# A one-layer streaming encoder step: when the sample tokens' cross attention, one spreading of a norm and the last norm's scalings are issued

## The chip, the core and the metric

The kernel runs on one core of a Trainium2 chip. The core has a matrix engine (TensorE, PE in the profile, with its weight loads as PEld), a vector engine (DVE), a scalar engine (ACT), a general engine (POOL) and a queue engine that only issues transfers (SP). ACT and POOL can issue transfers too. Each engine works through its own list of instructions in order and waits on semaphores for the others. The metric is the time of one execution on the device, in microseconds (us); lower is better. Three runs of the kernel before have a median of 2162.29 us (2162.05 to 2165.18).

## What is computed

One layer over 1024 prompt tokens and 64 sample tokens (1088 columns in all, D_MODEL 1024): a combined projection, retention and sliding-window attention as two gated branches, a mixing projection, cross attention over 256 memory tokens with 4 heads, a SwiGLU, and a final RMSNorm. What the change touches, cut from the reference:

```python
def rms_norm(x, g=None):
    xf = x.astype(jnp.float32)
    y = xf * lax.rsqrt(jnp.mean(xf * xf, axis=-1, keepdims=True) + EPS)
    if g is not None:
        y = y * g.astype(jnp.float32)
    return y.astype(x.dtype)
...
# x += CrossAttn(RMSNorm(x), memory K/V)   (4 heads, 256 memory tokens)
# x += SwiGLU(RMSNorm(x)), then a final RMSNorm
```

The prompt tokens attend to keys and values projected from the prompt's memory; the sample tokens attend to keys and values from a cache.

## The kernel before, in words

Activations lie with features on the 128 partitions and tokens along the columns. Matrix products are made of fp32r halves: a value is split into a rounded high part (an ACT copy, L124) and the remainder (a DVE subtraction, L125), and each block takes three multiplications (high by high, high by low, low by high: L157 to L159, or L223 to L226 in the large products). A scheduler orders each engine's list; `issue_after` and `in_order` pin an instruction behind the last multiplication, so what is emitted after a product comes after it on TensorE. `self.later` is a list of small steps; `run_later` (L169) empties it after the next product. So whoever appends to `self.later` gets its work placed between two products.

**Cross phase** (`cross_phase`, `attend`). `attend(h)` runs over the heads. It queues the loads of two query weight blocks (`raw`, split to `wq`) and of this head's memory keys and values (`mraw`, split to `mkv`), and then walks `CQ`, the chunks of 256 prompt columns; one chunk has 64 further columns, the sample tokens. A chunk is: two query products (`pd`), the scaled queries (`qf`, split to `cqs`), scores (`css`), softmax (`small_softmax`, L1297 to L1304), four transpositions (`cpt`, copied to `cpT`), the weighted values (`cpo`), and the split of those into `co`. After the last chunk of a head, L1350 to L1369 attend for the sample tokens: the cached keys and values `ck` and `cv` are loaded, scores `csss` (L1355), softmax to `ps`, two transpositions `cpts` (L1360), a DVE copy `cpTs` (L1362), and `cpos` (L1366), whose split goes to `co`. After the last head the output projection reads `co`.

**The norm behind it.** The norm ahead of the SwiGLU needs the factor of every token spread over the partitions. `spread_both` (L364) does this with 12 multiplications by the identity (L369) into a pair of banks, which ACT copies to `rstd_f` (L372, two copies). It is the first of the steps in `self.later` when `gate_up` makes its first large product through `plain` (L246). That product is four quarters of 24 multiplications each; three quarters have their first parts, then their second parts, and the steps run after the third second part (L262). The fourth quarter follows, on the operand `b`.

**Finish** (`finish`, L1702). The last projection's remaining half runs as 16 products of 9 multiplications: column groups c = 0 and c = 1, 272 columns each, with 8 row blocks each. c = 2, the other 544 columns, is done already. After each product `grow` adds it to the residual on DVE (L1721) and squares the result on ACT (L1725); `gather` adds the square of the product before on DVE (L1730). `sums` adds the squares over partitions by multiplications with ones (L1739), `roots` makes the factors in small DVE steps with one ACT square root (L1824 to L1831), `spread` lays them over the partitions (L1757, copied by ACT at L1761 where `copied`). `scale` multiplies a row block by gain and factor in one DVE instruction (L1767) and stores it; `gain` and `aside` do the same in two halves, the gain on ACT (L1772) and the factor on POOL (L1776).

Of the kernel before, what the change touches and what calls it, by code (L numbers as in the profile page):

```python
# [11 lines left out]
F32 = mybir.dt.float32  # L12
# [7 lines left out]
P = 128  # L20
# [89 lines left out]
class Kernel:  # L110
# [132 lines left out]
    def plain(self, w, x, emit, early=None, second=None):  # L243
# [14 lines left out]
        for i, t in emits:  # L258
            out.append(part(i, t, 1))
            if second is not None and len(out) == 1:  # L260
                second(emit(i, t, out[0], None))
# [1022 lines left out]
    def cross_phase(self):  # L1284
        nc, tc, io = self.nc, self.tc, self.io
        mm = nc.tensor.matmul
        with ExitStack() as ctx:
# [17 lines left out]

            def attend(h):
# [10 lines left out]
                for c0, n in CQ:  # L1317
# [32 lines left out]
                ck, cv = t2("ck"), t2("cv")  # L1350
                self.load(ck, io["cmkT"][h])
                self.load(cv, io["cmv"][h])
                pss = pc.tile([P, 2, 256], F32, tag="s", bufs=2, name="csss")
                for dt in range(2):
                    mm(pss[:SMP, 0, :], qsm[:, dt, :], ck[:, dt, :], start=dt == 0, stop=dt == 1)  # L1355
                p = t2("ps")
                small_softmax(pss, SMP, 1, p)
                pt = pc.tile([P, 2, 256], F32, tag="t", bufs=1, name="cpts")
                for kt in range(2):
                    nc.tensor.transpose(pt[:, kt, :SMP], p[:SMP, 0, kt * P:(kt + 1) * P], self.ident[:SMP, :SMP])  # L1360
                pT = cp.tile([P, 2, SMP], F32, tag="pTs", bufs=1, name="cpTs")
                nc.vector.tensor_copy(pT, pt[:, :, :SMP])  # L1362
                po = pc.tile([P, 2, 256], F32, tag="o", bufs=2, name="cpos")
                for dt in range(2):
                    for kt in range(2):
                        mm(po[:, dt, :SMP], cv[:, kt, dt * P:(dt + 1) * P], pT[:, kt, :], start=kt == 0, stop=kt == 1)  # L1366
                for dt in range(2):
                    o = outs[h][dt]
                    self.split(po[:, dt, :SMP], o[:, 0, SEQ:T], o[:, 1, SEQ:T])  # L1369
# [332 lines left out]
    def finish(self, y, rest):  # L1702
# [29 lines left out]
        def sums(c, *more):  # L1732
# [4 lines left out]
            for i, (a, w) in enumerate(spans):  # L1737
                for j, x in enumerate(parts):
                    self.last_mm = nc.tensor.matmul(ps[:, i, :], x[:, a:a + w], self.ones[:, :2], start=j == 0,  # L1739
                                                    stop=j == len(parts) - 1).ins  # L1740
# [28 lines left out]

        def gain(c, k):  # L1770
# [7 lines left out]

        for j in range(2 * KT):
# [23 lines left out]
        spare = [rest[i][0] for i in range(KT - 4, KT - 1)]  # L1803
        scale(0, 0, pb0)
        scale(0, 1, pb0)
# [96 lines left out]
```

## Time and profile before

| | us |
|---|---|
| Median of 3 runs | 2162.29 |
| The profiled execution's own time | 2162.52 |
| Its span | 2160.7 |
| Mean granted TensorE clock in it | 0.997 |
| PE busy | 2134.5 |
| DVE busy | 1552.6 |
| ACT busy | 874.8 |
| POOL busy | 530.4 |

A row of the timeline has the start in us from the span's start, the length in us, the engine, the line, the operation, output and inputs, their shape, and how many instructions were put together (x). Brackets give the idle time of that engine just before and what ended it. Matmuls overlap, so the distance from one start to the next, not the length, is what one costs. The view of waits sums such idle time by what ended it.

The cross phase lies at about 1168 to 1345 us, the spreading at 1449 us, the finish at 2121 us to the end.

### The profile page before, as it was taken

Reading aid. Unit: us, or ns where it says so; the run is one execution under the profiler, and the core shown is the slowest. Engines: PE = TensorE matmul, PEld = TensorE weight load, DVE = VectorE, ACT = ScalarE, POOL = GpSimd, SP = SyncE. Lnnn points to the kernel's source line nnn. Section 1 sums busy time; section 2 is a strip of 40 time slices with the busy share of each in tenths; the row PEclk is TensorE's granted clock in tenths of the full one; section 3 lists DMA queues with packets and bytes.
Section 4 is the critical chain, followed back from the end, with each engine's and each line's share of the span. In section 5 each row is a group of like instructions: output and inputs, shape, how many; then the busy total and the mean of one; then the engine's idle time right before and its main releaser. Section 6 shows DMA issues by size and latency. Waiting matters only on the chain.

```text
span 2160.7 us, 41729 instructions
## 1 busy us (share of the span) xinstructions
PE 2134.5 (99%) x16371; PEld 2082.7 (96%) x16371; DVE 1552.6 (72%) x2912; ACT 874.8 (40%) x1894; POOL 530.4 (25%) x448
## 2 busy tenths in 40 slices
PE   9999999999999999999999999999999999999997
PEld 9999999999999997889999999999999999999997
DVE  8987979776677567656455555677777777777597
ACT  8344434344444356543233333343223222334243
POOL 0000000022343135540000000015565556423531
PEclk9999999999999999999999999999999999999998
DMA  7334444435345485336442122413342332484333
GB/s 262 126 126 123 129 145 134 128 114 160 113 140 190 158 260 184 120 116 207 142 142 78 50 64 68 145 58 105 123 147 91 101 132 82 132 298 158 106 116 113
DMA packets 169893, 290.85 MB, mean 135 GB/s; under 512 B 39266, under 2 KB 96546, under 8 KB 169698
## 3 DMA queue, kind: packets, MB, share of 16 engines
q1 hardware_dynamic: 161666, 269.02, 38.8%
q0 software_dynamic: 3424, 10.82, 1.4%
q10 hardware_dynamic: 4608, 8.36, 1.0%
q8 instruction: 129, 2.11, 0.4%
q14 instruction: 66, 0.54, 0.1%
HBM read 196.97 MB, written 91.16 MB: 133 GB/s over the span
## 4 chain that ended last, share of the span: by engine, by line
PE 85%; DVE 7%; DMA 3%; issue 2%; ACT 2%; POOL 1%; SPq 0%; POOLq 0%; DVEq 0%; ACTq 0%
PE pq L226 17%; PE pq L224 16%; PE pq L223 16%; PE pd L157 8%; PE pd L159 8%; PE pd L158 8%; DVE wq L125 2%; DMA hl<-d_op 1%; PE pss L1005 1%; PE pout L1075 1%; DVE T L125 1%; PE pk L766 1%; PE pp L1051 1%; DVE B L125 1%; PE po L159 1%
## 5 line engine op out<-in xcount | busy, mean ns | idle before, releaser
L124 ACT CAST wq<-raw 128x512 fp32r<-128x512 f32 (+1 forms) x499 | 302.0, 614 | 564.7 <-PE pq L226 220.1
L125 DVE TENSOR_TENSOR wq<-raw,wq 128x512 fp32r<-128x512 f32 (+1 forms) x499 | 426.6, 859 | 137.3 <-ACT wq L124 133.9
L224 PE MATMUL pq<-T,wq 128*128 128x272 f32 x1832 | 492.1, 288 | 0.5 <-DVE T L125 0.5
L223 PE MATMUL pq<-T,wq 128*128 128x272 f32 x1832 | 490.4, 287 | 1.6 <-ACT wq L124 0.6
L224 PE MATMUL pq<-B,wq 128*128 128x272 f32 x1592 | 427.3, 288 | 1.9 <-DVE B L125 1.9
L223 PE MATMUL pq<-B,wq 128*128 128x272 f32 x1592 | 425.6, 287 | 0.2 <-ACT B L124 0.2
L226 PE MATMUL pq<-T,wq 128*128 128x272 f32 x1832 | 382.7, 289 | 1.9 <-DVE wq L125 1.9
L201 POOL TENSOR_TENSOR raw<-raw 128x512 f32<-128x512 f32 (+1 forms) x44 | 62.9, 1429 | 1260.5 <-DVE wq L125 527.6
L223 PEld LDWEIGHTS pq<-T,wq 128*128 128x128 f32 x1832 | 344.3, 188 | 3.2 <-ACT xsq L499 1.2
L224 PEld LDWEIGHTS pq<-T,wq 128*128 128x128 f32 x1832 | 343.9, 188 | 1.5 <-issue 0.7
L226 PE MATMUL pq<-B,wq 128*128 128x272 f32 x1592 | 331.9, 289 | 0.0
L224 PEld LDWEIGHTS pq<-B,wq 128*128 128x128 f32 x1592 | 298.9, 188 | 3.4 <-DVE B L125 3.0
L223 PEld LDWEIGHTS pq<-B,wq 128*128 128x128 f32 x1592 | 298.9, 188 | 0.7 <-ACT B L124 0.4
L226 PEld LDWEIGHTS pq<-T,wq 128*128 128x128 f32 x1832 | 289.6, 189 | 3.6 <-DVE wq L125 2.4
L226 PEld LDWEIGHTS pq<-B,wq 128*128 128x128 f32 x1592 | 251.7, 189 | 0.9 <-issue 0.7
L274 DVE TENSOR_TENSOR u<-pq,u 128x544 f32<-128x544 f32 x177 | 127.1, 718 | 76.0 <-PE pq L226 75.5
L613 DVE TENSOR_TENSOR stage<-pq,u 128x544 f32<-128x544 f32 x112 | 80.1, 717 | 32.5 <-PE pq L226 26.7
L157 PE MATMUL pd<-xc,wq 128*128 128x256 f32 (+1 forms) x256 | 74.5, 291 | 0.0
L159 PE MATMUL pd<-xc,wq 128*128 128x256 f32 (+1 forms) x256 | 74.0, 289 | 0.0
L158 PE MATMUL pd<-xc,wq 128*128 128x256 f32 (+1 forms) x256 | 73.7, 288 | 0.0
L1550 POOL TENSOR_TENSOR stage<-stage,rstd_f 128x544 f32<-128x544 f32 x40 | 63.9, 1608 | 39.1 <-ACT stage L1549 39.1
L204 POOL TENSOR_TENSOR raw<-raw 128x512 f32<-128x512 f32 (+1 forms) x44 | 59.0, 1340 | 53.1 <-DVE wq L125 50.5
(388 smaller groups left out, 4508.9 us busy)
## 6 DMA issues: line engine op xcount, KB each, us to landing
hl<-d_op SPq DMA_DIRECT2D x85, 272.0 KB, 5.3
d_qkv<-stage SPq DMA_DIRECT2D x44, 272.0 KB, 2.3
d_op<-stage SPq DMA_DIRECT2D x44, 272.0 KB, 2.2
d_op<-ht SPq DMA_DIRECT2D x44, 272.0 KB, 3.3
raw<-w_gate SPq DMA_DIRECT2D x22, 512.0 KB, 3.5
raw<-w_up SPq DMA_DIRECT2D x22, 512.0 KB, 5.0
raw<-w_down SPq DMA_DIRECT2D x16, 512.0 KB, 4.8
d_gate<-stage ACTq DMA_DIRECT2D x28, 272.0 KB, 2.8
```

The lines of the kernel that those rows point to most:

```text
L124: self.last_cast = self.nc.scalar.copy(hi, src).ins
L125: return self.nc.vector.tensor_tensor(out=lo, in0=src, in1=hi.bitcast(F32), op=ALU.subtract).ins
L157: mm(ps, wh, xh, start=start, stop=False)
L158: mm(ps, wh, xl, start=False, stop=False)
L159: self.last_mm = mm(ps, wl, xh, start=False, stop=stop).ins
L201: tt(out=a11, in0=a11, in1=a21, op=sub)
L223: mm(ps[:, c, :HC], w[:, 0, ks], x[:, 0, cs], start=start, stop=False)
L224: mm(ps[:, c, :HC], w[:, 0, ks], x[:, 1, cs], start=False, stop=False)
L226: self.last_mm = mm(ps[:, c, :HC], w[:, 1, ks], x[:, 0, c * HC:(c + 1) * HC], start=False, stop=stop).ins
L274: add = lambda out, a, b: nc.vector.tensor_tensor(out=out, in0=a, in1=b, op=ALU.add)
L613: nc.vector.tensor_tensor(out=o, in0=ps, in1=sb, op=ALU.add)
L1550: nc.gpsimd.tensor_tensor(out=g, in0=g, in1=r[t], op=ALU.mult)
```

## The change

Three edits, all of them about when and where work is done.

- **Sample tokens.** `attend` no longer ends with the sample tokens' attention. A new function `sample(h, qsm)` loads `ck` and `cv` and puts three steps into `self.later`, one after the other: scores and softmax, transpositions and copy, weighted values. Each comes after the next query product. `ck`, `cv` and `ps` get a buffer of their own each, where before they took turns in a ring of four. The last head walks its chunks in another order, so that chunks are left behind its sample columns.
- **Spreading.** `plain` runs the steps once more, after the second of the three second parts.
- **Finish.** In `sums` all spans of one operand come before those of the next. From the tenth of the sixteen products on, `gather` of the product before stands ahead of `grow` instead of behind it. Of the eight row blocks of c = 2, DVE scales four within the loop (before: seven) and a fifth after it; three are done by ACT and POOL early in the loop (before: one, at the loop's end). Of c = 0, the last two row blocks go to ACT and POOL, for which ACT also copies the spread factors. Their stores are issued by POOL. The ACT gains of c = 1 come later.

```diff
@@ plain
             out.append(part(i, t, 1))
+            if early is not None and second is None and len(out) == 2:
+                with self.tc.issue_after(self.last_mm):
+                    self.run_later()
...
@@ cross_phase
+            def sample(h, qsm):
+                ck, cv, p = (cp.tile([P, 2, 256], F32, tag=t, bufs=1, name=t) for t in ("ck", "cv", "ps"))
+                self.load(ck, io["cmkT"][h])
+                self.load(cv, io["cmv"][h])
+
+                def scores():
+                    pss = pc.tile([P, 2, 256], F32, tag="s", bufs=2, name="csss")
...
+                    small_softmax(pss, SMP, 1, p)
+                    behind(turn)
+
+                def turn():
...
+                    nc.vector.tensor_copy(pT, pt[:, :, :SMP])
+                    behind(lambda: weigh(pT))
+
+                def weigh(pT):
...
+                behind = lambda f: self.later.append(lambda: self.in_order(f))
+                behind(scores)
...
-                for c0, n in CQ:
+                for c0, n in CQ if h < H - 1 else CQ[3:] + CQ[:3]:
...
+                        sample(h, qsm)
...
-                ck, cv = t2("ck"), t2("cv")
-                self.load(ck, io["cmkT"][h])
...
-                    self.split(po[:, dt, :SMP], o[:, 0, SEQ:T], o[:, 1, SEQ:T])
@@ finish
-            for i, (a, w) in enumerate(spans):
-                for j, x in enumerate(parts):
...
+            steps = [(x, i, a, w) for x in parts for i, (a, w) in enumerate(spans)]
+            for j, (x, i, a, w) in enumerate(steps):
...
+        def turn(j):
+            if (j - 1) % KT and j:
+                gather((j - 1) // KT, rest[(j - 1) % KT][0])
...
+        held = (KT - 2, KT - 1)
         for j in range(2 * KT):
             c, m = divmod(j, KT)
             ps = self.in_order(lambda: product(c, *rest[m]))
+            if j > KT + 1:
+                turn(j)
             grow(c, rest[m][0], ps)
-            if (j - 1) % KT and j:
-                gather((j - 1) // KT, rest[(j - 1) % KT][0])
+            if j <= KT + 1:
+                turn(j)
...
-                pb0 = self.in_order(lambda: spread(0, False))[:, :HC]
-            if c and m < KT - 1:
-                scale(2, m)
-            if c and KT - 5 < m < KT - 1:
-                gain(1, rest[m][0])
-            if j == 2 * KT - 2:
-                gain(2, KT - 1)
-                aside(2, KT - 1)
+                pb0 = self.in_order(lambda: spread(0))[:, :HC]
+                gain(1, spare[0])
+                for k in held:
+                    aside(0, k, nc.gpsimd)
+            if c and m in (0, 1, 2, 4):
+                scale(2, min(m, 3))
+            if c and 0 < m < 4:
+                gain(2, KT - 4 + m)
+                aside(2, KT - 4 + m, nc.gpsimd)
+            if c and 4 <= m < 6:
+                gain(0, held[m - 4])
...
         scale(0, 1, pb0)
+        scale(2, KT - 4)
         self.in_order(lambda: sums(1, squares[1, m]))
         roots(1, lambda: scale(0, 2, pb0))
-        for k in range(3, KT):
+        for k in range(3, held[0]):
             scale(0, k, pb0)
```

What this does to the engines' lists, at three places. The numbers behind names tell tiles of one name apart.

On TensorE, at the end of the first head's last chunk, the instructions before (the next head's first product follows `cpos`):

```order
 L159 MATMUL pd<-xc_13014,wq 128x256
-L1338 MATMUL cpt<-ident,p 128x128
-L1355 MATMUL csss<-ck,qsm 64x256 x2
-L1338 MATMUL cpt<-ident,p 128x128 x3
...
-L1360 MATMUL cpts<-ident,ps 128x64 x2
-L1366 MATMUL cpos<-cpTs,cv 128x64 x4
```

In the changed kernel the two `csss` stand further up, among that chunk's `css`, `cpo` and `pd` rows, `cpts` stands inside the next head's products, and `cpos` some 50 rows behind `cpts`. Between the second `csss` and the first `css` of the next head lie 51 rows. On SP, whose loads start in order, this piece of the difference is the loads between the first and the third head:

```order
 L118 DMA ck<-cmkT 128x512
-L118 DMA cv<-cmv 128x512
 L118 DMA mraw<-d_mk 128x512
 L118 DMA mraw<-d_mv 128x512
+L118 DMA cv<-cmv 128x512
 L118 DMA raw<-w_cq 128x1024
 L118 DMA raw<-w_co 128x1024
```

The load of `ck` in its first row is the second head's now (before: the first head's). With one buffer for `ck` it waits until the first head's `csss` have read theirs, and the next head's `mraw` stands behind it; `cv` waits likewise for `cpos`.

On TensorE in `gate_up`'s first product, around the spreading (L369 before, L372 of the changed kernel). It moves from behind the 24 multiplications of the third second part (operands `B_16831` and `B_16832`) to ahead of them:

```order
 L226 MATMUL pq<-B_16830,wq 128x272 x2
+L372 MATMUL pq<-ident,rs_r 128x128 x6
 L223 MATMUL pq<-B_16831,wq 128x272
...
 L226 MATMUL pq<-B_16832,wq 128x272 x2
-L369 MATMUL pq<-ident,rs_r 128x128 x6
 L223 MATMUL pq<-b_15869,wq 128x272
```

On DVE in the finish, from the last `scale` of c = 2 within the loop to the sum for c = 1, before:

```order
-L1767 SCALAR_TENSOR_TENSOR y_22086<-y_22086,gains,rstd 128x544
-L1721 TENSOR_TENSOR y_22087<-pq,y_22087 128x272
-L1730 TENSOR_TENSOR rstd<-rstd,sq 128x272
-L1767 SCALAR_TENSOR_TENSOR y_22087<-y_22087,gains,rstd 128x544
-L1721 TENSOR_TENSOR y_22088<-pq,y_22088 128x272
-L1730 TENSOR_TENSOR rstd<-rstd,sq 128x272
-L1767 SCALAR_TENSOR_TENSOR rstd_f<-rstd_f,gains,pq 128x272
```

and the same stretch now (L1746 is `gather`, L1737 `grow`, L1783 `scale`):

```order
+L1746 TENSOR_TENSOR rstd<-rstd,sq 128x272
+L1737 TENSOR_TENSOR y_22087<-pq,y_22087 128x272
+L1746 TENSOR_TENSOR rstd<-rstd,sq 128x272
+L1737 TENSOR_TENSOR y_22088<-pq,y_22088 128x272
+L1783 SCALAR_TENSOR_TENSOR rstd_f<-rstd_f,gains,pq 128x272
+L1783 SCALAR_TENSOR_TENSOR y_22084<-y_22084,gains,pq 128x272
+L1783 SCALAR_TENSOR_TENSOR y_22085<-y_22085,gains,rstd 128x544
```

The scalings of 544 columns between the additions are gone, and each `gather` stands ahead of the next `grow`. POOL's list for the finish now reads:

```order
L1796 TENSOR_TENSOR y_22086<-y_22086,rstd 128x544 [waits DVE_49,Activation_49]
L1796 TENSOR_TENSOR y_22087<-y_22087,rstd 128x544
L1796 TENSOR_TENSOR y_22088<-y_22088,rstd 128x544 [waits PE_49]
L1797 DMA o_y<-y_22086 128x544 [waits Pool_49]
L1797 DMA o_y<-y_22087 128x544 [waits DMASW7_49,Pool_49]
L1797 DMA o_y<-y_22088 128x544 [waits Pool_49]
L1796 TENSOR_TENSOR y_22087<-y_22087,rstd 128x272 [waits Activation_49]
L1796 TENSOR_TENSOR y_22088<-y_22088,rstd 128x272
L1797 DMA o_y<-y_22087 128x272 [waits Pool_49]
L1797 DMA o_y<-y_22088 128x272 [waits DMASW2_49,Pool_49]
L1796 TENSOR_TENSOR y_22085<-y_22085,rstd 128x272 [waits Activation_49]
```

Before, it had one multiplication of 544 columns and three of 272 there, and no stores.

More of the change, by code (lines that the diff above doesn't have):

```diff
@@ L1349, in attend @@
                         self.split(po[:, dt, :], o[:, 0, c0:c0 + 256], o[:, 1, c0:c0 + 256])
-                ck, cv = t2("ck"), t2("cv")
-                self.load(ck, io["cmkT"][h])
[L1352 to L1368, printed above, removed]
-                    self.split(po[:, dt, :SMP], o[:, 0, SEQ:T], o[:, 1, SEQ:T])
             for h in range(H):
@@ L1736, in sums @@
             parts = [self.rstd[:, cols[c]], *more]
-            for i, (a, w) in enumerate(spans):
-                for j, x in enumerate(parts):
-                    self.last_mm = nc.tensor.matmul(ps[:, i, :], x[:, a:a + w], self.ones[:, :2], start=j == 0,
-                                                    stop=j == len(parts) - 1).ins
+            steps = [(x, i, a, w) for x in parts for i, (a, w) in enumerate(spans)]
+            for j, (x, i, a, w) in enumerate(steps):
+                self.last_mm = nc.tensor.matmul(ps[:, i, :], x[:, a:a + w], self.ones[:, :2], start=j == 0,
+                                                stop=j == len(steps) - 1).ins
             r = self.np.tile([P, 5], F32, tag="rf", bufs=2, name="rs_f")[:, :len(spans)]
@@ L1777, in aside @@
             queue.dma_start(self.io["o_y"][k, :, cols[c]], o)
+        spare = [rest[i][0] for i in range(KT - 4, KT - 1)]
+        held = (KT - 2, KT - 1)
         for j in range(2 * KT):
```

16 lines of the change are left out of this document (15 added, 1 removed).

## The prediction

> **What bounds the kernel now.** I read the page first, then the view of TensorE's waits from the cross phase on, then the timelines of the three places that the edits touch.
>
> ```profile
> span 2160.7 us, 41729 instructions
> PE 2134.5 (99%) x16371; PEld 2082.7 (96%) x16371; DVE 1552.6 (72%) x2912; ACT 874.8 (40%) x1894; POOL 530.4 (25%) x448
> PE 85%; DVE 7%; DMA 3%; issue 2%; ACT 2%; POOL 1%; SPq 0%; POOLq 0%; DVEq 0%; ACTq 0%
> ```
>
> TensorE sets the time: it is busy for all but 26 us of the span and has 85% of the chain that ended last. The change removes no multiplication, so it can only win where TensorE stands still, and behind its last product. The waits show how much there is to win:
>
> ```profile
> PE pq L1739 <- DVE rstd L1730: 2.4, 1, 2.4
> PE cpos L1366 <- DVE cpTs L1362: 1.7, 4, 0.6
> PE pq L1757 <- DVE rs_f L1831: 1.3, 1, 1.3
> PE pq L223 <- ACT rstd_f L372: 0.9, 1, 0.9
> PE cpo L157 <- ACT cpT L124: 0.7, 1, 0.7
> PE cpo L158 <- DVE cden L1302: 0.3, 1, 0.3
> ```
>
> Each row is a wait in total us, how often it came, and its longest. The first and third belong to the finish (3.7), the fourth to the spreading (0.9), the others to the cross phase (2.7). Together 7.3 us, 0.34% of the time: nothing that this change does can win much more. What a measurement of this kernel can tell from no change is about 0.2%, or 4.3 us.
>
> **Cross phase.** This is the sample tokens' block of the first head, then `cpos` of the second, and the first instruction behind the last head's.
>
> ```profile
> 1215.51 0.39 PE L157 MATMUL cpo<-cpT,mkv 128*128 128x256 f32 x1 [0.73 <-ACT cpT L124]
> 1217.41 0.28 PE L158 MATMUL cpo<-cpT,mkv 128*128 128x256 f32 x1
> 1217.53 0.28 PE L159 MATMUL cpo<-cpT,mkv 128*128 128x256 f32 x1
> 1217.74 0.34 PE L1360 MATMUL cpts<-ident,ps 64*128 64x64 f32 x2
> 1218.65 1.10 PE L1366 MATMUL cpos<-cpTs,cv 128*128 128x64 f32 x8 [0.58 <-DVE cpTs L1362]
> 1258.81 1.10 PE L1366 MATMUL cpos<-cpTs,cv 128*128 128x64 f32 x8 [0.38 <-DVE cpTs L1362]
> 1343.08 0.41 PE L157 MATMUL pd<-co,wq 128*128 128x320 f32 x1 [0.30 <-ACT co L124]
> ```
>
> `cpos` waits for the copy of the transpositions just ahead of it, with nothing between: 0.58 in the first head, 0.38 in the second, and 1.7 in all four. In the first head the sample softmax also sits in front of `cden` and `cpT` on DVE and ACT, which costs the 0.73 and, by the view of waits, 0.3. In the changed kernel some 50 multiplications of 0.12 us (the distance of the two plain `cpo` rows) lie between `cpts` and `cpos`, 6 us against a wait of at most 0.58, so these waits go in the first three heads: 0.73 + 0.3 + 0.58 + 0.38 + 0.38 = 2.4. The last head has no next head to hide in; its chunks change places so that some follow the sample's, but its last `co` must still come out before the projection, and I let its 0.38 and 0.30 stay, in another form. A new cost: the first head's `csss` now stand in two places instead of one. The step from a full array to another shape shows in the distance from 1217.53 to 1217.74, 0.21 against 0.12; there and back that is 0.2. Sum: **-2.2**. Bounds: only the waits on `cpTs` of three heads go (1.34 less 0.2, -1.1), or the last head's 0.68 go too (-2.9).
>
> The loads move too: the next head's `mraw` now stands on SP behind `ck`, which waits for `csss`. By the rows below the landing takes 2.7, the cast 0.62, and the subtraction behind it I take to be as long: the keys are there some 4 us behind `csss`, 4.3 with the issue.
>
> ```profile
> L124 ACT CAST mkv<-mraw x6: 619/622/622, 1217.1 to 1299.2; 128x512 fp32r<-128x512 f32 x6
> DMA to landing us min/median/max: 2.5/2.7/3.0
> ```
>
> The first scores that need them come 51 instructions later, 6.0 us: hidden by 1.7 us. Without that cover it would cost 4.3 us a head. The values `mv` are issued next and needed later still; `cv` waits for the `cpos` of the head before, ahead of weight loads that are a head away.
>
> **Spreading.** The product's third second part is the 24 multiplications from 1446.13 to 1449.12; then come the 12 of the spreading, and the operand-`b` quarter waits until ACT has copied them out.
>
> ```profile
> 1443.85 0.16 DVE L329 TENSOR_TENSOR rs_r<-rs_r,root 128x3 f32<-128x3 f32 x1
> 1446.13 0.29 PE L223 MATMUL pq<-B,wq 128*128 128x272 f32 x1
> 1444.68 2.55 ACT L124 CAST T<-xg 128x544 fp32r<-128x544 f32 x4 [4.06 <-DVE xg L1434]
> 1449.12 1.50 PE L369 MATMUL pq<-ident,rs_r 128*128 128x128 f32 x12
> 1450.65 0.81 ACT L372 COPY rstd_f<-pq 128x384 f32<-128x384 f32 x2 [0.66 <-PE pq L369]
> 1451.51 0.39 PE L223 MATMUL pq<-b,wq 128*128 128x272 f32 x1 [0.90 <-ACT rstd_f L372]
> ```
>
> The factors are ready at 1444.0, so the spreading can start at 1446.13, as the change places it, and end at 1447.6. ACT is through its casts at 1447.2, so the copies end at about 1448.4. The quarter starts at 1446.13 + 1.50 (the spreading) + 2.99 = 1450.6, 2 us later: the wait of 0.90 goes, and with it what the first instruction after a wait takes more (0.39 against 0.29). I take **-1.0**, which is also the better bound. The worse is 0: the copies now stand ahead of casts of `T` and weights that the next product needs, and may give back there what they won.
>
> **Finish.** Here the aim is to relieve DVE, which is late by 2 us behind the last product:
>
> ```profile
> 2145.25 0.29 PE L159 MATMUL pq<-T,wb 128*128 128x272 f32 x1
> 2147.45 0.43 DVE L1730 TENSOR_TENSOR rstd<-rstd,sq 128x272 f32<-128x272 f32 x1
> 2147.94 0.59 PE L1739 MATMUL pq<-ones,rstd 128*128 128x2 f32 x2 [2.40 <-DVE rstd L1730]
> 2150.70 0.16 DVE L1824 TENSOR_SCALAR rf_v<-pq 128x3 f32<-128x3 f32 x1 [2.00 <-PE pq L1739]
> 2151.99 1.65 PE L1757 MATMUL pq<-ident,rs_f 128*128 128x128 f32 x6 [1.33 <-DVE rs_f L1831]
> 2143.59 0.83 PE L1757 MATMUL pq<-ident,rs_f 128*128 128x128 f32 x6
> ```
>
> Three scalings of 0.70 leave DVE's loop, 2.1 us. But POOL takes two more, and POOL and DVE get in each other's way:
>
> ```profile
> 2135.23 0.39 ACT L1761 COPY rstd<-pq 128x288 f32<-128x288 f32 x1
> 2135.69 1.37 POOL L1776 TENSOR_TENSOR y<-y,rstd 128x544 f32<-128x544 f32 x1 [24.33 <-ACT rstd L1761]
> 2136.70 0.66 DVE L1730 TENSOR_TENSOR rstd<-rstd,sq 128x272 f32<-128x272 f32 x1
> 2138.34 0.77 DVE L1767 SCALAR_TENSOR_TENSOR y<-y,gains,rstd 128x544 f32<-128x544 f32 x1
> 2141.13 0.14 DVE L1824 TENSOR_SCALAR rf_v<-pq 128x3 f32<-128x3 f32 x1
> 1448.38 0.71 DVE L125 TENSOR_TENSOR T<-xg,T 128x544 fp32r<-128x544 f32 x1
> 1456.60 5.80 DVE L125 TENSOR_TENSOR T<-xg,T 128x544 fp32r<-128x544 f32 x4
> 1456.19 4.99 POOL L1550 TENSOR_TENSOR g<-g,rstd_f 128x544 f32<-128x544 f32 x3 [12.39 <-ACT g L1549]
> ```
>
> The same `gather` takes 0.43 alone and 0.66 where POOL's multiplication still runs: it ends 0.3 after POOL does. Further up, four subtractions that take 0.71 singly took 5.80 while POOL did three multiplications. They take turns. So I play the changed lists through. ACT's copy ends at about 2136.1 (one gain of 0.5 now stands ahead of it). POOL's three run 2136.1 to 2137.4, then in turn with one DVE instruction each, to about 2141.1. DVE's `gather` ends at 2137.8, its first scaling at 2139.8 and its second at 2141.8, against 2139.1 in the trace. Five further instructions (2.1) bring `rf_v` of c = 0 to about 2143.9, 2.8 later. The three scalings no longer there would win 2.1 back, but the last three products now go `grow`, square, `gather` in turn, 1.2 us each (0.35 + 0.5 + 0.35 by their starts, with the hand-over), where DVE cannot run ahead, and POOL's two multiplications of 272 columns fall among them. The last `grow` comes out at 2149.5 to 2149.8, its square at 2150.2; the old list's last `gather` ended at 2147.9. The reordered `sums` need only their second half behind that square: 0.65 at full clock, 1.3 at half. So `rf_v` stands at 2150.9 to 2152.2, +0.2 to +1.5 against 2150.70.
>
> Which clock decides in part, and this view shows it:
>
> ```profile
> 2146.00:2148.00 2.00, 0.06 (x1) 0.06 (x1) 2.00 (x6) 1.38 (x3) 0.00 (x0) 0.99 0.36 139
> 2148.00:2150.00 2.00, 2.00 (x10) 2.00 (x10) 0.70 (x2) 0.00 (x0) 0.00 (x0) 0.50 0.74 262
> ```
>
> The groups are TensorE, its loads, DVE, ACT and POOL, and the next number is the granted clock: it halved after 2.4 us of idleness. In the changed kernel the products end later too, at about 2147.1 (they wait for banks that DVE frees), and the sums start 2.3 us behind: an even chance. The Trainium skill, TensorE: Matmul & The Clock Gate, Part 1, puts the halving behind an idle stretch of some 3.4 us; the trace halved earlier, and the measurement decides. At full clock the spreading at the end is also 0.8 shorter (1.65 against 0.83). So the finish lies between -0.6 and +1.5; I take **+0.5**, the middle. ACT's added work (two gains of 0.75, two of 0.5, one copy of 0.4) fits: it is busy 1.38 of 2 us in the fuller of these two stretches. The stores that pass from SP's queue to POOL's start over 5 us before the end, and behind them on POOL stand only the last three multiplications, which wait for the last spreading; they cost nothing unless POOL is still at them at 2153.
>
> That the loser of the two engines waits for a whole instruction, if its own has two SBUF inputs, is what the Trainium skill states too (SBUF — State Buffer, Who interferes with whom), and the rows above agree; it speaks against this edit.
>
> **Sum.** -2.2 - 1.0 + 0.5 = -2.7, on the profiled execution's own 2162.52: 2159.8. That execution lies 0.23 above the median, so 2159.6. With the bounds of the parts, this case's own range is 2158.0 to 2161.4.
>
> **Rivals.** (1) The finish wins as meant: POOL's work costs DVE little, because the scalings meet it in gaps. For it: additions that read `pq` are not held up in the trace, and they are half of DVE's list. Against it: the 0.66 and the 5.80. Then the 2.1 are won, less 1.2 for a last product that waits its turn, and the last `grow` comes 0.9 earlier; the sums' second half starts some 1.5 us behind the last product at full clock and takes 0.65, so `rf_v` stands at 2148.2 (-2.5) and the spreading is 0.8 shorter: -3.3. Total -6.5, 2155.8. (2) The sample steps don't win: the waits return at new places, since two chunks' scores, softmaxes and transpositions now share DVE and ACT with the sample's. For it: `cpT` and `cden` already came last once. Against it: DVE has gaps of some us there. Cross phase 0: 2161.8. (3) Slower: `mraw` behind `ck`. The cover is 1.7 us; from a landing of 4.4 us on, TensorE waits in each of three heads. At a landing of 7 us that is 2.6 each, 7.8 in all: 2167.4. For it: one in-order queue now has a wait on TensorE in it. Against it: the landings were 2.5 to 3.0.
>
> **Chances.** Forecast 0.50, rival (1) 0.33, (2) 0.11, (3) 0.06. The predicted time is 2159.6. The range reaches down over most of (1) and up over (2): 2155.4 to 2162.2. Faster by over 0.2% (below 2157.97): nearly all of (1) and a tenth of the forecast's low end, 0.40. Slower: 0.06. Within: 0.54.
>
> **What would show it.** Cross phase: no row of `cpos` or `cpo` waiting in the first three heads; a row of `css` waiting for `mkv` speaks for (3). Spreading: no wait of `pq<-b`. Finish: the scalings on DVE at 2137 to 2142 take over 1.5 us each, and the sums' start, at 2149 or later (less what was won ahead of it), against 2147 in rival (1). The prediction is wrong if the finish ends over 1 us earlier by itself, or if the cross phase wins less than 1.

## The result, and the profile after

The changed kernel has a median of 2158.07 us over 22 runs (2154.89 to 2162.25), against 2161.56 us over 22 runs of the kernel before (2157.72 to 2165.18). The ratio of the times is 0.9987, with a 95% interval of 0.9981 to 0.9993: 2.8 us less, between 1.5 and 4.1. It is not the ratio of the two medians, which lie 3.5 us apart, inside the same interval; gains in time go by the ratio from here on. The interval leaves no doubt that the change is faster, but the gain is within the 0.2% that was called no change. 2159.6 had been forecast.

Runs of one kernel lie up to 8 us apart within one measurement, so a gain of 1 us is not read from the times. The profile can be cut into parts, however, and most parts are steady where the whole is not. These are the borders in the changed kernel's timeline: the first product of the cross phase, the first large product behind it, the first product on operand `b`, and the factors of c = 2 in the finish.

```profile
1169.84 0.28 PE L157 MATMUL pd<-xc,wq 128*128 128x256 f32 x1
1430.77 0.29 PE L223 MATMUL pq<-B,wq 128*128 128x272 f32 x1
1450.75 0.29 PE L223 MATMUL pq<-b,wq 128*128 128x272 f32 x1
2129.11 0.16 DVE L1853 TENSOR_SCALAR rf_v<-pq 128x5 f32<-128x5 f32 x1
```

Before, the same four stood at 1167.29, 1430.49, 1451.51 and 2132.52. So the cross phase went from 263.20 to 260.93 (-2.27), the stretch with the spreading from 21.02 to 19.98 (-1.04), and the finish, from its border to the end of the span, from 28.2 to 29.2 (+1.0). The parts with an edit give -2.3 in sum. What lies between them scatters: the cross phase's first product comes anywhere from 1166.4 to 1170.6 us in the profiles below, whatever the edit.

The page's head, and six of the ten rows in the view of TensorE's waits from the cross phase on (total, times, longest):

```profile
span 2158.3 us, 41692 instructions
PE 2136.2 (99%) x16371; PEld 2085.5 (97%) x16371; DVE 1549.7 (72%) x2908; ACT 877.6 (41%) x1899; POOL 541.3 (25%) x457
```

```profile
PE pq L1755 <- DVE rstd L1746: 2.3, 1, 2.3
PE pq L1773 <- DVE rs_f L1860: 1.3, 1, 1.3
PE pq L157 <- DVE y L1737: 0.6, 1, 0.6
PE pd L157 <- ACT co L124: 0.5, 1, 0.5
PE pq L157 <- DVE rstd_f L1737: 0.4, 1, 0.4
PE pd L157 <- DVE qf L1356: 0.4, 1, 0.4
```

No wait of `cpos` or `cpo` is left, and none of `pq<-b`. The last head has two waits of 0.5 and 0.4 in place of 0.38 and 0.30. The finish keeps its two waits of 2.3 and 1.3. TensorE now waits for `grow` too (0.6, `y` at L1737), for a bank that DVE has not emptied. The 0.4 for `rstd_f` is not the edit's: it lies ahead of the factors of c = 2, and e1 and e2 below, with the old finish, have 0.32 and 0.35 there.

These are rows from the timeline of DVE and POOL in the finish, with the factors of c = 0 and c = 1:

```profile
2133.29 0.99 DVE L1746 TENSOR_TENSOR rstd<-rstd,sq 128x272 f32<-128x272 f32 x1
2134.21 1.90 DVE L1783 SCALAR_TENSOR_TENSOR rstd_f<-rstd_f,gains,rstd 128x544 f32<-128x544 f32 x1
2136.38 1.51 DVE L1783 SCALAR_TENSOR_TENSOR y<-y,gains,rstd 128x544 f32<-128x544 f32 x1
2139.91 0.15 DVE L1853 TENSOR_SCALAR rf_v<-pq 128x3 f32<-128x3 f32 x1
2143.95 0.54 DVE L1746 TENSOR_TENSOR rstd<-rstd,sq 128x272 f32<-128x272 f32 x1 [0.50 <-ACT sq L1741]
2145.33 0.44 DVE L1746 TENSOR_TENSOR rstd<-rstd,sq 128x272 f32<-128x272 f32 x1 [0.49 <-ACT sq L1741]
2148.59 0.16 DVE L1853 TENSOR_SCALAR rf_v<-pq 128x3 f32<-128x3 f32 x1 [0.96 <-PE pq L1755]
2132.61 4.70 POOL L1796 TENSOR_TENSOR y<-y,rstd 128x544 f32<-128x544 f32 x3 [24.89 <-ACT rstd L1777]
```

While POOL works from 2132.61 to 2137.3, DVE's `gather` takes 0.99 (0.43 alone; before, at this place and behind POOL's one multiplication, 0.66), and its scalings take 1.90 and 1.51 (before 0.77). The factors of c = 0 come 10.80 us behind those of c = 2; before it was 8.61 (2141.13 - 2132.52). From there to the factors of c = 1 it is 8.68 (before 9.57), and to the end 9.7 (before 10.0). So +2.2, -0.9 and -0.3.

### The profile page after: what moved, and what is told of

Read it like the earlier page. It is cut to its first block, busy times and chain, and to the rows that moved or that the text cites. A ratio compares the mean times of both kernels' runs of the same rounds, so it can differ in the third digit from the quotient of the medians.

```text
span 2158.3 us, 41692 instructions
## 1 busy us (share of the span) xinstructions
PE 2136.2 (99%) x16371; PEld 2085.5 (97%) x16371; DVE 1549.7 (72%) x2908; ACT 877.6 (41%) x1899; POOL 541.3 (25%) x457
## 3 DMA queue, kind: packets, MB, share of 16 engines
q10 hardware_dynamic: 4608, 8.36, 1.0%
## 4 chain that ended last, share of the span: by engine, by line
PE 87%; DVE 6%; DMA 3%; ACT 2%; issue 2%; POOL 1%; SPq 0%; POOLq 0%; DVEq 0%; ACTq 0%
PE pq L226 17%; PE pq L224 17%; PE pq L223 17%; PE pd L157 8%; PE pd L158 8%; PE pd L159 8%; DVE wq L125 1%; PE pout L1078 1%; PE pss L1008 1%; DVE T L125 1%; PE pk L769 1%; PE pp L1054 1%; PE po L157 1%; PE po L159 1%; PE po L158 1%
## 5 line engine op out<-in xcount | busy, mean ns | idle before, releaser
L616 DVE TENSOR_TENSOR stage<-pq,u 128x544 f32<-128x544 f32 x112 | 80.4, 720 | 30.4 <-PE pq L226 25.8
```

The source lines that it names most:

```text
L616: nc.vector.tensor_tensor(out=o, in0=ps, in1=sb, op=ALU.add)
```

## The experiments

All parts in us, from the starts of the same four borders in each kernel's timeline (cross phase; spreading; finish, as c = 2 to c = 0, c = 0 to c = 1, and on to the end). The ratio is that of the times to those of before, with its interval.

| | cross | spreading | c2 to c0 | c0 to c1 | to end | finish | ratio |
|---|---|---|---|---|---|---|---|
| before | 263.2 | 21.0 | 8.60 | 9.57 | 10.0 | 28.2 | 1 |
| the change | 260.9 | 20.0 | 10.80 | 8.68 | 9.7 | 29.2 | 0.9987 [0.9981, 0.9993] |
| e1 only the sample steps | 260.0 | 21.0 | 8.60 | 8.75 | 10.0 | 27.4 | 0.9987 [0.9979, 0.9996] |
| e2 only the spreading | 263.0 | 20.0 | 8.60 | 8.36 | 10.0 | 27.0 | 0.9998 [0.9989, 1.0007] |
| e3 only the finish | 263.1 | 21.0 | 10.77 | 7.72 | 9.7 | 28.2 | 1.0009 [1.0000, 1.0017] |
| e4 without the finish | 260.9 | 20.0 | 8.60 | 8.36 | 10.0 | 27.0 | 0.9996 [0.9987, 1.0004] |
| e5 the change again | 260.9 | 20.0 | 10.78 | 8.67 | 9.7 | 29.1 | 0.9996 [0.9987, 1.0004] |
| e6 POOL's three left out | 260.0 | 20.0 | 8.37 | 8.17 | 9.3 | 25.8 | 0.9993 [0.9985, 1.0002] |
| e7 idle multiplications | 260.9 | 20.0 | 10.81 | 7.65 | 9.0 | 27.4 | 0.9993 [0.9985, 1.0002] |
| e8 sums on TensorE | 260.0 | 20.0 | 8.60 | 7.45 | 10.0 | 26.1 | 0.9986 [0.9977, 0.9994] |
| e9 gather behind grow | 259.8 | 20.0 | 10.78 | 6.71 | 9.1 | 26.6 | 0.9983 [0.9974, 0.9992] |
| e10 combination a | 260.9 | 20.0 | 8.94 | 8.11 | 9.8 | 26.8 | 0.9988 [0.9979, 0.9996] |
| e11 combination b | 260.9 | 20.0 | 9.34 | 7.59 | 9.6 | 26.5 | 0.9974 [0.9963, 0.9984] |
| e12 combination c | 260.9 | 20.0 | 8.93 | 6.71 | 10.7 | 26.3 | 0.9969 [0.9956, 0.9981] |

**Each edit alone.** e1 to e3 have one of the three diffs each, e4 the first two.

> Only the sample steps are moved. Measured from the cross phase's first product to the first product on operand b, which was 284.2 us before and 280.9 us after, with both other edits out. Theory (the moved steps win what TensorE waited in the sample blocks): 282.0, 2.2 less than before, no wait on cpTs, cpT or cden left, and the time 2.2 us below before. Rival (the shorter stretch is luck of one execution, or comes from the spreading): 284.2 and the same time. The finish stays at 40.1 us from its first product to the end.

> Only the spreading is moved. Theory: the wait of 0.90 before the product on operand b is gone and nothing waits behind it, the same stretch is 283.2 us, 1.0 less than before. Rival (the copies that now stand ahead of casts give it back): a wait of TensorE for T or wq of up to 1 us within 15 us behind the spreading, stretch and time as before. A second question that all four of these runs bear on: before had 2.7 us of waits for B on DVE between 1900 and 1995 us that the changed kernel's profile has not. Theory: they come and go with the execution, whatever the edit. Rival: an edit removes them, and they are missing from every run that has it.

> Only the finish is changed. Theory (POOL's multiplications hold DVE up): from the finish's first product to the end 41.3 us as in the changed kernel, 1.2 more than the 40.1 of before, and the time 1.2 us above before. Rival (the finish wins by itself, and the changed profile's finish was late for other reasons): 37 us, and the time 3 us below before.

> Sample steps and spreading as changed, the finish as before. Theory: 280.9 us for the stretch to operand b, 40.1 us for the finish, the time 3.3 us below before and so 1.2 us below the whole change. Rival (the three edits need each other, or the finish wins): 1 us or more above the whole change.

The parts move with their edits. The cross phase is 263.0 to 263.2 in the three kernels without the sample steps and 260.9 or less in all others; the spreading's stretch is 21.0 without its edit and 20.0 with it, and no later wait for T or `wq` shows in e2. By the times e1 is lower (0.9 to 4.5 us), e3 higher (0 to 3.7), e2 not to be told from before; e4's interval (-2.8 to +0.9) does not quite hold the -3.3 of its two parts. e1's stretch to operand `b` is 281.0, 1.0 less than its theory had: in that profile the output projection ran faster, as it did in four of the eleven profiles with this edit and not in the other seven (last section). What lies between the parts is in the time too: in e4's profile the cross phase starts 2.1 us later than in that of before. For the finish I measured in the expectations from its first product, which turned out to carry a wait that varies (0.75 to 1.47 in e2, e3, before and the change); from the factors of c = 2 on, the new finish costs c = 0 2.2 us in every execution (e3's 10.77).

The second question of e2: the waits for B near 1900 us were 1.9 us in the view of waits before and 0 in the changed kernel; they were 1.8 in e2, 2.0 in e4, 0.5 in e3 and e5, and 0 in e1, e6, e10 and e12. The change and e5 are one kernel, and e4 has them with two edits. So no edit by itself takes them away or brings them, and they go with the execution.

**The change again** (e5).

> The whole change once more, unaltered. Measured: the parts of the span by their borders on TensorE. Theory (each part is set by the kernel, but the clock behind the last product and the waits for B near 1900 us come by chance): 280.9 us from the cross phase's first product to operand b, the factors of c = 0 at 22.9 us behind the finish's first product, as in the other executions that have the edits; the finish 39.5 to 41.4 us. Rival (the parts themselves scatter): either of the first two differs by over 0.3.

The parts come back to 0.1. The time does not: -0.9 by the ratio, against -2.8 in the first measurement, with intervals (-4.1 to -1.5 and -2.8 to +0.9) that overlap.

**What POOL costs** (e6): in the finish,

```diff
-            nc.gpsimd.tensor_tensor(out=o, in0=o, in1=self.rstd[:, cols[c]], op=ALU.mult)
+            if c < 2:
+                nc.gpsimd.tensor_tensor(out=o, in0=o, in1=self.rstd[:, cols[c]], op=ALU.mult)
```

> The whole change, but POOL leaves out its three multiplications of 544 columns (row blocks 5 to 7 of c = 2 are stored without the factor), everything else in place. Theory (POOL's multiplications hold up DVE's instructions with two SBUF inputs): DVE's gather and first two scalings behind them take 0.43, 0.77 and 0.77 instead of 0.99, 1.90 and 1.51; the factors of c = 0 start 2.2 us earlier, at 20.7 behind the finish's first product, and the time is 2 us below the whole change. Rival (the new order of gather and grow is what makes the finish late): 22.9, and the same time.

DVE's rows at the same place of the list, now with POOL at rest:

```profile
2130.26 0.43 DVE L1746 TENSOR_TENSOR rstd<-rstd,sq 128x272 f32<-128x272 f32 x1
2130.61 0.78 DVE L1783 SCALAR_TENSOR_TENSOR rstd_f<-rstd_f,gains,rstd 128x544 f32<-128x544 f32 x1
2131.66 0.78 DVE L1783 SCALAR_TENSOR_TENSOR y<-y,gains,rstd 128x544 f32<-128x544 f32 x1
```

0.99, 1.90 and 1.51 are back to 0.43, 0.78 and 0.78, and c = 0 comes 2.4 earlier (10.78 to 8.37). So the theory of POOL is right. The finish is 3.3 shorter, but that is not POOL's price alone: in e6 the clock stayed full through the sums (behind a pause of TensorE of 1.79 and not 2.30), and in e5 it was halved. Against e3, whose sums ran at nearly full clock, the finish is 2.4 shorter (28.2 to 25.8), and against e7 below, with a full clock to its end, 1.6. That is about the 2 us that I gave it. By the time alone it would not have shown.

**The clock** (e7): idle multiplications into columns of the sums' bank that nobody reads, ahead of the last sums.

```diff
+            if more:
+                for _ in range(9):
+                    self.last_mm = nc.tensor.matmul(whole[:, 128:256], self.ident, self.ident, start=True, stop=True).ins
```

> The whole change, with nine idle multiplications of the identity placed on TensorE between the last product and the sums. Theory (the halved clock behind 2.3 us of idleness makes sums and spreading slow): the granted clock stays at 1.0 to the end, the sums' second half takes 0.7 instead of 1.4, the last spreading 0.83 instead of 1.65, together 1.5 us off the finish where the clock would have halved. Rival (the sums are late because of DVE, and the clock is no matter): nothing, or later where the idle multiplications stand in the way.

First two windows of the changed kernel around its sums (the number behind POOL's group is the granted clock) and the timeline of its last sums and spreading, then the same of e7:

```profile
2144.00:2146.00 2.00, 0.17 (x1) 0.17 (x2) 1.50 (x4) 1.42 (x3) 2.00 (x4) 0.96 0.16 63
2146.00:2148.00 2.00, 2.00 (x11) 2.00 (x11) 1.63 (x4) 0.43 (x1) 0.18 (x1) 0.50 0.64 219
```

```profile
2147.13 1.42 PE L1755 MATMUL pq<-ones,sq 128*128 128x2 f32 x6
2149.88 1.65 PE L1773 MATMUL pq<-ident,rs_f 128*128 128x128 f32 x6 [1.33 <-DVE rs_f L1860]
```

```profile
2142.00:2144.00 2.00, 1.95 (x18) 1.75 (x16) 1.50 (x6) 1.27 (x3) 1.70 (x3) 1.00 0.15 57
2144.00:2146.00 2.00, 0.99 (x8) 0.83 (x7) 1.93 (x8) 0.31 (x2) 0.00 (x0) 1.00 0.68 222
```

```profile
2144.16 0.83 PE L1759 MATMUL pq<-ones,sq 128*128 128x2 f32 x6
2146.36 0.94 PE L1777 MATMUL pq<-ident,rs_f 128*128 128x128 f32 x6 [1.37 <-DVE rs_f L1864]
```

The clock stays at 1.00, the sums' second half takes 0.83 for 1.42, the spreading 0.94 for 1.65, and the finish is 1.7 us shorter than e5's (27.43 against 29.13). As expected; but not all of the 1.7 is due to the filling. The clock changes only at steps 3.41 us apart (last section), and in e7 such steps fall at 2144.60 and 2148.01, so that most of the sums would have run at full clock anyway. e3 has the same finish without the filling, and there too the last product ended just ahead of a step (0.25 us; 0.13 in e7): its sums ran at nearly full clock, its spreading at half, and its finish took 28.2. Against that one the filling won 0.8.

**Sums on TensorE** (e8): the finish as before, but

```diff
-            if (j - 1) % KT and j:
+            if (j - 1) % KT and j < 2 * KT - 2 and j:
...
-        self.in_order(lambda: sums(1, squares[1, m]))
+        self.in_order(lambda: sums(1, *(squares[1, rest[i][0]] for i in range(KT - 3, KT))))
```

with the sums in the changed order, operand by operand.

> Sample steps and spreading as changed; the finish as before, but the last two gathers of c = 1 are left to TensorE: sums takes the squares of the last three row blocks besides the gathered ones, operand by operand. Theory (behind the last product DVE's list is the bound): DVE is rid of 0.7, and the sums need only three multiplications behind the last square, so the last factors start 2.4 us earlier at full clock and 1.5 at half than with the finish of before (27 to 28.6 us behind the finish's first product, against 28.3 to 30.1), and the time is 5 us below before. Rival: the squares keep their buffers longer and ACT waits for one; no gain.

TensorE's timeline behind the last product:

```profile
2138.15 0.29 PE L159 MATMUL pq<-T,wb 128*128 128x272 f32 x1
2138.27 0.72 PE L1755 MATMUL pq<-ones,rstd 128*128 128x2 f32 x6
2138.86 1.53 PE L1755 MATMUL pq<-ones,sq 128*128 128x2 f32 x12
2140.60 0.83 PE L1755 MATMUL pq<-ones,sq 128*128 128x2 f32 x6 [0.21 <-ACT sq L1741]
```

The sums follow the last product at once, and the wait of 2.40 is 0.21. c = 0 to c = 1 takes 7.45 against 8.36 at full clock (e2, e4) and 9.57 at half. The end gains no more than that, as DVE's five scalings of c = 0 still stand between the last factors and c = 1. Theory right at 0.9 to 2.1, a little under what I had given it (1.5 to 2.4); the time went 3.0 below before by the ratio (1.3 to 5.0), where 5 had been expected.

**The order of gather** (e9): the whole change, with `gather` behind `grow` everywhere.

```diff
-            if j > KT + 1:
-                turn(j)
             grow(c, rest[m][0], ps)
-            if j <= KT + 1:
-                turn(j)
+            turn(j)
```

> The whole change, but gather stands behind grow for all products, as before. Theory (ahead of grow it makes DVE wait for a square on each of the last products, 0.5 twice): no wait of DVE for a square between the last products; the last grow starts about 1 us earlier, and the last factors 0.3 us earlier, since both halves of the sums then stand behind the last gather: 17.9 to 19.2 us behind the factors of c = 2, against 19.5 (halved clock) and 18.5 (full). Rival (the order pays, because half of the sums may start early): the last factors come 0.5 or more later.

The last `grow` and `gather` on DVE, the sums on TensorE, and the window in which they begin:

```profile
2141.55 0.43 DVE L1737 TENSOR_TENSOR y<-pq,y 128x272 f32<-128x272 f32 x1
2141.90 0.65 DVE L1746 TENSOR_TENSOR rstd<-rstd,sq 128x272 f32<-128x272 f32 x1
2142.60 0.83 PE L1755 MATMUL pq<-ones,rstd 128*128 128x2 f32 x6 [1.81 <-DVE rstd L1746]
2143.29 0.81 PE L1755 MATMUL pq<-ones,sq 128*128 128x2 f32 x6
```

```profile
2141.00:2143.00 2.00, 0.40 (x4) 0.40 (x4) 2.00 (x6) 1.54 (x4) 2.00 (x4) 1.00 0.30 115
```

I had the sign and missed the size: the last factors come 17.5 behind those of c = 2, not 17.9 to 19.2. The two waits of 0.50 and 0.49 for squares are gone, TensorE is idle for 1.81 and not 2.30, and this time the clock held, so all of the sums ran at full speed. Against e7, where the clock held with `gather` ahead, the order alone is worth 0.8 (27.43 to 26.62); the rest of the 2.5 against e5 goes with the clock. Whether the shorter pause kept the clock up or the place of the steps did (last section) is not shown.

**Combinations** (e10 to e12). e10 is e8 with the last two row blocks of c = 0 on POOL and five idle multiplications ahead of the last spreading; e11 is e10 with one scaling of c = 2 moved behind the last `grow`.

```diff
-        pb = self.in_order(lambda: spread(1))[:, :HC]
+        pb = self.in_order(lambda: spread(1, idle=5))[:, :HC]
...
+                for k in (KT - 2, KT - 1):
+                    gain(0, k)
+                    aside(0, k, nc.gpsimd)
```

```diff
-            if c and m < KT - 1:
+            if c and m < KT - 2:
                 scale(2, m)
...
+        scale(2, KT - 2)
         scale(0, 0, pb0)
```

> Sample steps, spreading and the sums on TensorE; besides, the last two row blocks of c = 0 on POOL as in the change, and five idle multiplications ahead of the last spreading. Theory: full clock in the last spreading (0.83 instead of 1.65) and two scalings fewer on DVE behind the last factors, so DVE begins c = 1 0.8 us earlier than with the sums on TensorE alone: from the factors of c = 2 to the end 25.3 us instead of 26.07, time 0.8 us lower. Rival (POOL's two multiplications hold up the scalings of c = 2 by as much): 26 us or more.

> As the one before, with one scaling of c = 2 moved behind the last grow, where DVE waits for the sums. Theory: the last grow 0.7 us earlier, the last factors 0.5 to 0.7 earlier, 24.7 us from the factors of c = 2 to the end. Rival (DVE's work behind the last product is the bound, whatever its order): 25.3 us, as the one before.

Both came out longer than e8 in the finish (26.8 and 26.5 against 26.1). In e10 the rival was right; e11 lies 0.3 below e10, between its theory (0.6 less) and its rival (the same). In e10, by DVE's timeline, the scaling that met POOL's two multiplications took 1.28 and the next one 0.93, and the clock fell all the same, while the five idle multiplications ran (a granted clock of 0.67 in their window, and 1.48 for the last spreading):

```profile
2139.20 1.28 DVE L1785 SCALAR_TENSOR_TENSOR y<-y,gains,rstd 128x544 f32<-128x544 f32 x1
2140.76 0.93 DVE L1785 SCALAR_TENSOR_TENSOR y<-y,gains,rstd 128x544 f32<-128x544 f32 x1
```

e12 starts from the whole change, with the order of e9 and the sums of e8, and with two of POOL's three row blocks back on DVE:

```diff
-            if c and 0 < m < 4:
-                gain(2, KT - 4 + m)
-                aside(2, KT - 4 + m, nc.gpsimd)
+            if c and m == 3:
+                gain(2, KT - 1)
+                aside(2, KT - 1, nc.gpsimd)
...
+        for k in (KT - 3, KT - 2):
+            scale(2, k)
```

> The whole change with three things undone or altered in the finish: gather behind grow, POOL keeps one multiplication of 544 columns for c = 2 as before (DVE does row blocks 5 and 6 behind the last factors), and the squares of the last three row blocks of c = 1 go to the sums on TensorE. Theory (POOL's extra multiplications and the order of gather were what the new finish lost by; DVE's work behind the last factors is then the bound): the factors of c = 0 8.6 us behind those of c = 2 (10.8 in the change), those of c = 1 6.0 to 6.7 behind them, the end 10.2 later, 25 us in all against 29.1 in the change and 27.0 to 28.2 before; the time 5 us below before. Rival (the finish hangs on one of these alone): 26.5 us or more, as in the three runs that altered one.

c = 0 to c = 1 is 6.71, as expected, but the end came 10.7 behind and not 10.2, and the finish is 26.3. The two scalings of c = 2 that I put there met POOL once more, as the timelines of the two engines show:

```profile
2144.35 1.97 DVE L1783 SCALAR_TENSOR_TENSOR y<-y,gains,rstd 128x544 f32<-128x544 f32 x2
2144.70 2.95 POOL L1796 TENSOR_TENSOR y<-y,rstd 128x272 f32<-128x272 f32 x3 [3.40 <-ACT rstd L1777]
```

Its time, 2154.23 us (2152.95 to 2157.62, 6 runs) against 2160.69 us of before, has the lowest ratio of all: 0.9969, 6.7 us, with an interval of 4.1 to 9.5 us. Against the change it has 2.8 us less by the finish (26.3 against 29.1), while the intervals of the two ratios touch at 0.9981. It is not shown to be better than e8: e8's finish is 26.1, with its last spreading at half clock (1.65) where e12's ran at full (0.93), and the intervals of their ratios overlap.

## Why the prediction was right

- **Total.** -2.7 was forecast. 2.8 was measured (1.5 to 4.1), and by the three parts it is 2.3. The sum was right, with two of its terms on the point and one too low. That the total came within 0.1 is luck: the interval is 2.6 wide, and e5, the same kernel, gave 0.9. The forecast of 2159.6 also started from the 2162.29 of three runs; from the 2161.56 of all 22 it would have been 2158.9. And the range called this case's own, 2158.0 to 2161.4, is narrower than the bounds of the three parts: added up (-4.5 to +0.4) they give 2157.8 to 2162.7.
- **Cross phase, -2.2.** 2.27 in the changed profile, and TensorE's waits in this phase went from 3.0 to 0.9. The waits named are gone from the first three heads, the last head's stayed in another form (0.46 and 0.38), and the keys are not late: no `css` waits for `mkv`, so rival (3) had no room. Rival (2), that the waits return at new places, fell too.
- **Spreading, -1.0.** 1.04, and nothing given back behind it.
- **Finish, +0.5.** 1.0 with the clock halved in both profiles (28.2 to 29.2), 1.2 with it full, or nearly, in the sums of both (27.0 of e2 and e4, 28.2 of e3). The mechanism was right, row by row: POOL and DVE in turn, `gather` at 0.99 and two scalings over 1.5, c = 0 late by 2.2 where 2.8 was forecast, and the sums beginning 16.7 behind the factors of c = 2 (before 15.4), where 16.5 or more had been named as the sign (2149 against 2132.52). The size was low because I put the middle between a halved and a full clock. The clock at this place comes with the execution, before and after alike: in e2 and e4 it held through the sums behind an idle stretch of 2.40, in e3 it held nearly as long behind 2.30, and in both profiles of the whole change and in that of before it did not. A term that takes the better half of a chance for the changed kernel alone sets the two sides against each other unevenly.
- **Rival (1).** It asked what happens if POOL costs DVE little. e6 has that, with the multiplications left out: the finish is then 2.4 below before, against the 3.3 of the rival. Half of that is the clock, which was full in e6's sums and halved in those of before; against e2 and e4, with full sums, it is 1.2. So less was there to win than the rival had, and the turn-taking takes it.

What the prediction did not see: the new order of `gather` is itself a loss. I counted it as a limit on what the missing scalings can win (1.2 per product); that putting it back would win 0.8 I did not work out.

## What to carry to other kernels

- An instruction that is moved from one engine to a slower one which must take turns with it can cost the first engine more than it saves. Here a scaling of 0.70 on DVE became a multiplication of 1.3 or more on POOL, and three of these delayed DVE's chain by 2.4 (e6), 0.8 each. Look in the old trace for one place where both work at once before dealing anything out.
- A kernel whose runs scatter by 0.4% can still be judged part by part: cut the span at instructions that both versions have, and compare the parts that the edit touches. Most parts came back to 0.1 us here. Two did not, the cross phase (1.0 between equal lists) and the finish behind the last product (the clock), so take each kernel's profile more than once, and compare parts at the same clock.
- Behind the last product, an engine with a chain of grow, square and gather is better served by letting the matrix engine add the squares itself: it is idle there, and the pause of 2.40 became one of 0.21 (e8). It does not by itself keep the clock up: in e8 the clock fell right behind the sums, in e10 soon after.

## What the runs showed of the hardware that was not expected

**The clock changes on a fixed beat.** In the profile of before the sums began after 2.40 us of idleness at half clock. In e2 they began after the same 2.40 and ran at full (0.36 each against 0.56), and in e1 the clock fell in their midst:

```profile
2145.15 0.38 PE L1752 MATMUL pq<-ones,rstd 128*128 128x2 f32 x2 [2.39 <-DVE rstd L1743]
2145.84 0.36 PE L1752 MATMUL pq<-ones,sq 128*128 128x2 f32 x2
2146.06 0.56 PE L1752 MATMUL pq<-ones,rstd 128*128 128x2 f32 x2
```

So the length of the pause alone does not decide. Two profiles in which the clock changed more than once show when it can change. In e11 it did so at 2120.30, 2123.71 and 2144.19 us, which is 3.41 and then six times 3.41 apart. In e10 it did so at 2143.70, 2147.11 and 2150.52. These are e10's windows between those steps (TensorE's busy time is the first number behind the length, and the granted clock stands behind POOL's group):

```profile
2140.28:2143.70 3.42, 2.54 (x22) 2.37 (x22) 2.85 (x8) 1.47 (x4) 1.89 (x3) 1.00 0.65 244
2143.70:2147.11 3.41, 2.90 (x15) 2.60 (x13) 2.14 (x9) 0.51 (x2) 0.01 (x1) 0.50 0.70 222
2147.11:2150.52 3.41, 0.00 (x0) 0.00 (x0) 2.07 (x5) 0.00 (x0) 2.18 (x3) 1.00 0.66 228
```

If the steps are counted back from the fall in each profile, the stretch ahead of a step shows how busy TensorE was. Here are two such stretches in a row for e5, where the clock fell, for e9, where it held over the first step, and for e8:

```profile
2138.84:2142.25 3.41, 1.49 (x13) 1.26 (x11) 2.42 (x7) 2.73 (x7) 2.02 (x3) 1.00 0.21 82
2142.25:2145.66 3.41, 2.72 (x12) 2.64 (x12) 2.45 (x7) 0.91 (x3) 0.72 (x2) 0.50 0.59 205
```

```profile
2139.27:2142.68 3.41, 1.60 (x14) 1.38 (x12) 3.41 (x9) 2.89 (x8) 2.34 (x3) 1.00 0.28 108
2142.68:2146.09 3.41, 2.08 (x17) 1.99 (x18) 3.23 (x11) 0.38 (x2) 0.65 (x2) 1.00 0.77 266
```

```profile
2138.23:2141.65 3.42, 2.98 (x26) 2.81 (x24) 2.85 (x8) 1.81 (x4) 0.00 (x0) 1.00 0.69 262
2141.65:2145.06 3.41, 1.65 (x6) 1.35 (x6) 3.19 (x11) 0.59 (x2) 0.15 (x1) 0.50 0.58 187
```

With 1.49 us of products in such a stretch the clock fell at its end (e5). With 1.60 it held (e9, 0.08 of it the first sums), and with 1.64 it fell (e11, 2116.88 to 2120.30). In e2 it held with 1.81. So the border lies near half of a stretch and is not sharp in these numbers. The sums count for little: in e8 TensorE was busy for 2.98 us, all but 0.2 of it with them, and the clock fell. What matters at the end of this kernel is therefore where the last product ends on the beat. In before and in the change it ended 1.0 and 1.1 us behind a step, and the clock fell as the sums began; in e2 and e4 it ended 1.8 and 2.9 behind one, and the clock held through the sums. What places the beat in an execution is not shown.

By the Trainium skill, TensorE: Matmul & The Clock Gate, What's actually happening, the clock falls after an idle window of about 3.4 us, and the windows run freely. The steps 3.41 us apart agree with that. That a window has to be idle does not: in e5 the products filled 1.49 us of it, and the pause was 2.30.

**One stage ran at two speeds.** The cross phase with the sample steps took 260.9 in seven profiles and 259.8 to 260.0 in four (e1, e6, e8, e9). The difference lies in the output projection, whose multiplications of 384 columns last 336 ns in e1 and 339 in the changed kernel, by the groups of one line and shape (busy us, mean ns):

```profile
L158 PE MATMUL pd<-co,wq 128*128 128x384 f32 x112 | 37.7, 336 | 0.0
```

```profile
L158 PE MATMUL pd<-co,wq 128*128 128x384 f32 x109 | 37.0, 339 | 0.0
```

The lists of TensorE are the same there, the granted clock is 1.00 in both, and e6 and e5 differ only in the finish. What sets it stays open; it was not tried.
